# Softmax halves put off behind the next maximum, values between a second head's scores, and an early row load in an attention stage

## The chip, the cores and the metric

The kernel runs on one core of a Trainium2 chip. The metric is the device time of one execution in microseconds (us). A core has a matrix engine (PE), a vector engine (DVE, VectorE), a scalar engine (ACT, ScalarE), GpSimd (POOL) and a sync engine (SP) that here only issues transfers. Each engine works through its own list of instructions in order; semaphores order the engines among each other. Matmul results land in PSUM, which has eight banks of 128 partitions x 512 f32.

## What is computed

One inference step of two layers on 256 prompt tokens and 1024 latent tokens of width 1024. The first layer is a gated linear attention, the second a softmax attention with 8 heads over 2 key/value heads; the change lies in the second. Cut to what matters here:

```python
def attend_blocks(q, keys, vals):               # one block of 128 queries
    def one(qblk):
        s = jnp.einsum("bqhgd,bkhd->bhgqk", qblk, keys).astype(jnp.float32) * scale
        p = jax.nn.softmax(s, axis=-1).astype(vals.dtype)
        return jnp.einsum("bhgqk,bkhd->bqhgd", p, vals)

# layer 1, latent tokens: 1024 own keys and 256 cached ones
qs, ks_, vs, gs = attn_project(hs, att_w_in[i], att_qnorm[i], att_knorm[i])
out_s = (attend_blocks(rope_2d(qs), keys, vals) * jax.nn.silu(gs)) @ att_w_out[i]
xs = xs + gt_s * out_s
```

The prompt tokens do the same over their own 256 keys.

## The kernel before

Every f32 product is made of three f16 matmuls: an operand is split into a high and a low half, and hi x hi, hi x lo and lo x hi add up in one PSUM bank.

The attention stage (`attention`) runs 10 steps: two groups of four heads (p) times five column blocks c of 256 tokens. Block 0 holds the prompt (256 keys), blocks 1 to 4 the latent tokens (1280 keys). In each step the four heads e = 0 to 3 are taken in order, and each head has two halves j of 128 tokens. A score tile is one head's half: `scores` computes 128 x 1280 scores with nine matmuls into an S tile of three banks, of which there are two. Then come the maximum over the row (VectorE, line 977), its scaled negative (ScalarE, 979), the exponential with its row sum (ScalarE, 982), the reciprocal of the sum and that times 2**14 (VectorE, 984 and 986), the high half of the normalised row (GpSimd, 989), the low half (VectorE, 990), and one transposing transfer of both halves into PT, issued by SP (991). `values` multiplies a head's PT with the values, two heads late: a list `pend` holds the two heads that wait. The row buffers p and phl exist twice, PT three times.

Between the scores of an even head stands the projection of the next queries (`query`, 24 matmuls); its norm, rotary turn and split go to ScalarE, VectorE, GpSimd and SP, the second half of them in the odd head (`query_rest`). After an odd head, `gateT` computes the gate of both heads of the pair (2 x 24 matmuls), and its SiLU runs on ScalarE and VectorE (`silu`, `logsig`, lines 224 to 235). All these matmuls use two `mm` banks. So a pair of heads is four score tiles, one query projection, two `values` and two gates. The last step has no queries left to project.

`out2_prep` loads a block's finished attention rows back from DRAM (line 1086) and splits them for the output projection, with a maximum over the rows (1090), a small matmul that spreads it over the partitions (84), and the split on ScalarE (1097) and VectorE (1098). For the first output block it is called in the second head of the last step. After the loop come the first tile of the output projection (`out_tile`), the last two `values`, and `att_out` with the other nine tiles.

The engines' lists are not in the order of the program text: the framework's scheduler reorders independent instructions by a time model of its own, and `tc.issue_after(x)` holds the instructions of a block on x's engine behind x. In the code of before nothing in the attention stage is held in that way.

Before the attention stage, `gla_out` fills the PSUM with pools y, tr, mm and kv of two banks each, whose first banks are taken in the order y, tr, mm, kv (line 1309). The attention's pool is laid over the same eight banks: the two S tiles over the first six, its `mm` over the last two. A bank is reused when the old tile's last reader is through.

Of the kernel before, what the change touches and what calls it, by code (L numbers as in the profile page):

```python
# [16 lines left out]
P = 128  # L17
# [9 lines left out]
HD, AH, KVH = 128, 8, 2  # L27
# [16 lines left out]
OUT = (1, 0, 2, 3, 4)  # L44
# [8 lines left out]
class K:  # L53
# [907 lines left out]
    def scores(self, h, c, j, q, PT):  # L961
        nc = self.nc
        kv = h // (AH // KVH)
        nk = 256 if c == 0 else TS + PAST
# [12 lines left out]
        nc.vector.tensor_reduce(mx, S, AX.X, ALU.max)  # L977
# [4 lines left out]
        nc.scalar.activation(p, S, AF.Exp, scale=self.sexp, bias=nb, accum_out=den)  # L982
        r = self.t(self.sm, [P, 1], F32, "srec")
# [59 lines left out]
    def attention(self, wo):  # L1043
        self.S0 = self.t(self.ps, [P, 1536], F32, "S")
        wq, wg, q, g = self.wq, self.wg, self.q, {}
        pend, later = [], []
        for n, (p, c) in enumerate(self.steps):
# [8 lines left out]
            for e in range(4):  # L1056
                h = 4 * p + e
                if later:
                    self.nc.sync.dma_start(*later.pop(0))
                PT = self.t(self.sp, [P, 20, 256], F16, "PT", bufs=3)  # L1060
                self.scores(h, c, 0, q[(p, c, 0)], PT)
                if e % 2 == 0:
                    self.query()
                else:
                    self.query_rest()
                self.scores(h, c, 1, q[(p, c, 1)], PT)
                if len(pend) == 2:
                    self.values(*pend[0], g.pop(pend.pop(0)[0]))
                pend.append((h, c, PT))
                if e % 2 == 1:  # L1070
                    g.update({i: self.gateT(i, c, *wg[p]) for i in (h - 1, h)})
                if n == 9 and e == 1:
                    first = self.ropet.rearrange("p a b d -> p (a b d)").bitcast(F16)
                    first = first.rearrange("p (j h t) -> p j h t", j=2, h=AH)
                    self.prep = self.out2_prep(OUT[0], (first[:, 0], first[:, 1]))
# [7 lines left out]
    def out2_prep(self, c, parts):  # L1083
        nc = self.nc
        og = self.t(self.wst, [P, AH, 256], F32, "wst")
        nc.sync.dma_start(og, self.og2_d[c])
# [42 lines left out]
def emit(ctx, tc, I, O, dbg=None, stop=None):  # L1129
# [172 lines left out]
    with ExitStack() as ca:  # L1302
        k.ap = k.pool("ap", ctx=ca, side="right")
        with ExitStack() as c:
# [4 lines left out]
            k.held = {t: k.bank(t) for t in ("y", "tr", "mm", "kv")}  # L1309
# [110 lines left out]
```

## Time and profile before

| quantity | value |
| --- | --- |
| median of 3 runs (lowest, highest) | 1352.31 us (1348.84, 1357.2) |
| the profiled execution: its time | 1360.72 us |
| the profiled execution: its span | 1358.9 us |
| mean granted clock of the matrix engine | 0.978 |
| first score matmul of the attention stage | 784.83 us |
| first matmul of the output projection's second block | 1260.76 us |

The span is what the profile covers; the execution's time has 1.8 us around it. In the profile's lines a time is counted from the start of the span, a row of the timeline reads "start, duration, engine, line, operation, out<-in, shape", and in brackets at its end stands how long the engine sat idle before it and what released it. Lines name the tile, not its number. "PEld" is the load of a stationary operand, which runs beside the matmuls. Neighbouring matmuls overlap in the records, so the cost of one is read from start to start.

### The profile page before, as it was taken

How to read it: one execution, taken by the hardware profiler on the slowest of the kernel's cores; microseconds unless marked ns; L12 is line 12 of the kernel's file. 1: busy time of each engine (PE TensorE's matmuls, PEld its weight loads, DVE VectorE, ACT ScalarE, POOL GpSimd, SP SyncE). 2: the span in 40 equal slices, each digit the busy share in tenths (PEclk: the TensorE clock that was granted, in tenths of full speed). 3: DMA queues.
4: the chain of work that ended last, by engine and by line, in shares of the span. 5: the costliest groups of instructions: out<-in, count | busy, mean ns of one | idle time of the engine just before them, and what ended most of it. 6: DMA issues, size and time to landing. Idle time of an engine off the chain costs nothing. (4 is left out here: it accounts for less than half of the span.)

```text
span 1358.9 us, 22664 instructions
## 1 busy us (share of the span) xinstructions
PE 1245.7 (92%) x8150; PEld 808.9 (60%) x8150; DVE 931.1 (69%) x2138; ACT 669.7 (49%) x1661; POOL 382.8 (28%) x623
## 2 busy tenths in 40 slices
PE   4789999999999999697889989899999989989998
PEld 2357765655555556475657656666676756665444
DVE  1776868886867788755654567777768677875552
ACT  2565646655646567523323455555566555562110
POOL 1232212422322133401222534333233343422000
PEclk9899999999999999898989999999999989999999
DMA  9612455544545532377543268576859638887532
GB/s 306 219 62 95 140 178 182 168 154 133 187 132 178 160 113 78 101 214 198 129 127 121 60 181 155 104 137 121 188 102 188 128 83 145 182 156 171 174 132 78
DMA packets 344769, 199.14 MB, mean 147 GB/s; under 512 B 229406, under 2 KB 331534, under 8 KB 343376
## 3 DMA queue, kind: packets, MB, share of 16 engines
q1 hardware_dynamic: 297024, 159.67, 47.3%
q10 hardware_dynamic: 47312, 37.25, 8.5%
q8 instruction: 64, 1.05, 0.3%
q0 software_dynamic: 320, 0.77, 0.2%
q14 instruction: 49, 0.40, 0.1%
HBM read 104.31 MB, written 37.24 MB: 104 GB/s over the span
## 5 line engine op out<-in xcount | busy, mean ns | idle before, releaser
L125 PE MATMUL mm<-whi,hT_hi 128*128 128x512 f16 (+1 forms) x560 | 197.1, 352 | 12.1 <-ACT gx L471 7.4
L125 PEld LDWEIGHTS <-hT_hi 128*128 128x128 f16 x1440 | 142.2, 99 | 109.9 <-issue 15.4
L125 PE MATMUL mm<-wlo,hT_hi 128*128 128x512 f16 (+1 forms) x560 | 196.8, 351 | 0.0
L125 PE MATMUL mm<-whi,hT_lo 128*128 128x512 f16 (+1 forms) x560 | 196.6, 351 | 0.0
L125 PEld LDWEIGHTS <-whi 128*128 128x128 f16 x1368 | 135.5, 99 | 90.5 <-issue 21.7
L125 PE MATMUL mm<-hT_hi,whi 128*128 128x256 f16 (+1 forms) x512 | 155.2, 305 | 10.5 <-DVE og L1015 5.4
L989 POOL TENSOR_SCALAR phl<-p,srec 128x1280 f16<-128x1280 f32 (+1 forms) x80 | 99.9, 1250 | 218.7 <-DVE srec L984 146.2
L125 PE MATMUL mm<-hT_lo,whi 128*128 128x256 f16 (+1 forms) x512 | 155.5, 304 | 0.2 <-DVE hT_lo L350 0.2
L125 PE MATMUL mm<-hT_hi,wlo 128*128 128x256 f16 (+1 forms) x512 | 155.4, 304 | 0.0
L990 DVE SCALAR_TENSOR_TENSOR phl<-p,srec,phl 128x1280 f16<-128x1280 f32 (+1 forms) x80 | 107.5, 1344 | 59.0 <-POOL phl L989 58.9
L974 PE MATMUL S<-kT,wst 128*128 128x512 f16 (+1 forms) x624 | 122.9, 338 | 14.4 <-ACT p L982 14.4
L125 PE MATMUL mm<-PT,vh 128*128 128x256 f16 x672 | 113.7, 273 | 4.9 <-DMA PT<-phl 4.5
L977 DVE TENSOR_REDUCE smx<-S 128x1 f32<-128x1280 f32 (+1 forms) x80 | 101.0, 1267 | 3.3 <-PE S L974 3.3
L982 ACT ACTIVATE p<-S,snb,sexp 128x1280 f32<-128x1280 f32 (+1 forms) x80 | 99.3, 1241 | 5.0 <-DVE srec L984 1.1
L125 PEld LDWEIGHTS <-hT_lo 128*128 128x128 f16 x720 | 71.1, 99 | 49.7 <-issue 1.0
L974 PEld LDWEIGHTS <-wst 128*128 128x128 f16 x624 | 61.0, 98 | 65.8 <-issue 16.2
L125 PEld LDWEIGHTS <-wlo 128*128 128x128 f16 x720 | 71.3, 99 | 39.6 <-issue 2.8
L125 PE MATMUL mm<-PT,vl 128*128 128x256 f16 x336 | 91.6, 273 | 0.0
L125 PE MATMUL y<-whi,ogT 128*128 128x256 f16 (+1 forms) x336 | 76.6, 318 | 6.7 <-DVE xr L724 4.6
L147 DVE TENSOR_REDUCE wmx<-wst 128x1 f32<-128x512 f32 x104 | 64.5, 676 | 26.5 <-DMA wst<-in_gla_w_in 10.7
L979 ACT ACTIVATE snb<-smx,nsexp 128x1 f32<-128x1 f32 x80 | 23.4, 292 | 115.7 <-DVE smx L977 115.7
L125 PEld LDWEIGHTS <-vh 128*128 128x128 f16 x672 | 65.4, 98 | 15.0 <-issue 4.3
(335 smaller groups left out, 2696.8 us busy)
## 6 DMA issues: line engine op xcount, KB each, us to landing
wada<-in_w_ada SPq DMA_DIRECT2D x16, 1024.0 KB, 5.0
wst<-in_gla_w_in SPq DMA_DIRECT2D x12, 1024.0 KB, 5.8
wst<-in_att_w_in SPq DMA_DIRECT2D x10, 1024.0 KB, 8.3
xr<-x_d SPq DMA_DIRECT2D x11, 512.0 KB, 3.3
og_d<-gx ACTq DMA_DIRECT2D x40, 128.0 KB, 1.8
og_d<-og ACTq DMA_DIRECT2D x40, 128.0 KB, 3.8
wst<-og_d SPq DMA_DIRECT2D x5, 1024.0 KB
out<-xr ACTq DMA_DIRECT2D x17, 256.0 KB, 2.0
```

The source lines that it names most:

```text
L125: self.nc.tensor.matmul(out, a, b, start=k == 0 and j == 0, stop=k == n - 1 and j == 2)
L147: nc.vector.tensor_reduce(mx[:, j : j + 1], st[:, 2 * j : 2 * j + 2, :], AX.XY, ALU.max, apply_absolute_value=True)
L974: nc.tensor.matmul(S[:, a : a + n], x, y, start=m == 0, stop=m == 2)
L977: nc.vector.tensor_reduce(mx, S, AX.X, ALU.max)
L979: nc.scalar.activation(nb, mx, AF.Copy, scale=self.nsexp)
L982: nc.scalar.activation(p, S, AF.Exp, scale=self.sexp, bias=nb, accum_out=den)
L989: nc.gpsimd.tensor_scalar(hi, p, r, 2.0 ** 14, ALU.mult, ALU.mult)
L990: nc.vector.scalar_tensor_tensor(lo, p, r2, hi, ALU.mult, ALU.subtract)
```

## The change

The softmax of a score tile is cut in two. `scores` now ends with the exponential and keeps the rest (reciprocal, high half, low half, transposing transfer) in `self.put_off`; the next call of `scores` emits that rest behind its own maximum, held behind it on VectorE by `issue_after`. After the loop one last `rest()` takes the last tile. In an odd head the call of `values` moves from behind the second score tile to between the two. The load of the first output block is split off `out2_prep` (`out2_load`) and called in the first head of the last step; the rest of `out2_prep` is held behind the maximum of the second head's second tile. And `gla_out`'s banks are taken in the order y, tr, kv, mm, so that the attention's `mm` lies over the old `mm` and its second S tile over the old kv.

```diff
--- before.py
+++ after.py
@@ -974,12 +974,26 @@
                 nc.tensor.matmul(S[:, a : a + n], x, y, start=m == 0, stop=m == 2)
             a += n
         mx = self.t(self.sm, [P, 1], F32, "smx")
-        nc.vector.tensor_reduce(mx, S, AX.X, ALU.max)
+        last = nc.vector.tensor_reduce(mx, S, AX.X, ALU.max).ins
         nb = self.t(self.sm, [P, 1], F32, "snb")
         nc.scalar.activation(nb, mx, AF.Copy, scale=self.nsexp)
         p = self.t(self.sp, [P, TS + PAST], F32, "p")[:, 0:nk]
         den = self.t(self.sm, [P, 1], F32, "sden")
         nc.scalar.activation(p, S, AF.Exp, scale=self.sexp, bias=nb, accum_out=den)
+        self.rest(last)
+        self.last = last
+        self.put_off = p, den, PT, j, nk
+
+
+    def rest(self, after=None):
+        if self.put_off is None:
+            return
+        if after is not None:
+            with self.tc.issue_after(after):
+                return self.rest()
+        nc = self.nc
+        p, den, PT, j, nk = self.put_off
+        self.put_off = None
         r = self.t(self.sm, [P, 1], F32, "srec")
         nc.vector.reciprocal(r, den)
         r2 = self.t(self.sm, [P, 1], F32, "srec2")
@@ -1041,7 +1055,7 @@
             self.queries_out(self.half.pop(), 1)
 
     def attention(self, wo):
-        self.S0 = self.t(self.ps, [P, 1536], F32, "S")
+        self.S0, self.put_off = self.t(self.ps, [P, 1536], F32, "S"), None
         wq, wg, q, g = self.wq, self.wg, self.q, {}
         pend, later = [], []
         for n, (p, c) in enumerate(self.steps):
@@ -1061,18 +1075,24 @@
                 self.scores(h, c, 0, q[(p, c, 0)], PT)
                 if e % 2 == 0:
                     self.query()
+                    self.scores(h, c, 1, q[(p, c, 1)], PT)
                 else:
                     self.query_rest()
-                self.scores(h, c, 1, q[(p, c, 1)], PT)
                 if len(pend) == 2:
                     self.values(*pend[0], g.pop(pend.pop(0)[0]))
+                if e % 2 == 1:
+                    self.scores(h, c, 1, q[(p, c, 1)], PT)
                 pend.append((h, c, PT))
                 if e % 2 == 1:
                     g.update({i: self.gateT(i, c, *wg[p]) for i in (h - 1, h)})
+                if n == 9 and e == 0:
+                    row = self.out2_load(OUT[0])
                 if n == 9 and e == 1:
                     first = self.ropet.rearrange("p a b d -> p (a b d)").bitcast(F16)
                     first = first.rearrange("p (j h t) -> p j h t", j=2, h=AH)
-                    self.prep = self.out2_prep(OUT[0], (first[:, 0], first[:, 1]))
+                    with self.tc.issue_after(self.last):
+                        self.prep = self.out2_prep(row, (first[:, 0], first[:, 1]))
+        self.rest()
         gt = self.t(self.wst, [P, KT, 256], F32, "wst").rearrange("p (i k) n -> p i (k n)", i=2)
         self.fold_gate(1, wo[0][2] + wo[1][2], gt)
         wo[:] = [(hi, lo, 512) for hi, lo, _ in wo]
@@ -1080,10 +1100,13 @@
         for t in pend:
             self.values(*t, g.pop(t[0]))
 
-    def out2_prep(self, c, parts):
-        nc = self.nc
+    def out2_load(self, c):
         og = self.t(self.wst, [P, AH, 256], F32, "wst")
-        nc.sync.dma_start(og, self.og2_d[c])
+        self.nc.sync.dma_start(og, self.og2_d[c])
+        return og
+
+    def out2_prep(self, og, parts):
+        nc = self.nc
         hi, lo = parts
         mx = self.t(self.small, [P, 2], F32, "wmx")
         for j in range(2):
@@ -1113,7 +1136,7 @@
         w = self.wtile(0)
         for n, c in enumerate(OUT):
             if n + 1 < 5:
-                nxt = self.out2_prep(OUT[n + 1], [t[:, :, 256 * (n % 2) : 256 * (n % 2) + 256] for t in w[0:2]])
+                nxt = self.out2_prep(self.out2_load(OUT[n + 1]), [t[:, :, 256 * (n % 2) : 256 * (n % 2) + 256] for t in w[0:2]])
             for j in range(n == 0, 2):
                 x = self.t(self.xp, [P, D], F32, "xr")
                 self.out_tile(c, j, x, wo, (512, 256, 256) if (n, j) == (4, 1) else (512, 512))
@@ -1306,7 +1329,7 @@
             k.hw = k.pool("hw3", bufs=2, ctx=c)
             k.sm = k.pool("sm3", bufs=4, ctx=c)
             k.ps = k.pool("ps3", 2, PSUM, c)
-            k.held = {t: k.bank(t) for t in ("y", "tr", "mm", "kv")}
+            k.held = {t: k.bank(t) for t in ("y", "tr", "kv", "mm")}
             k.p2_bank = "kv"
             k.gla_out(wo, prep, (k.nw, k.w2))
         if "x1" in k.dbg:
```

No instruction is added to or taken from the arithmetic. What follows are rows of the engines' lists, of before and of the changed kernel.

VectorE, from the second head's first tile of one pair to the first tile of the next pair (step 1). Names: smx is a tile's maximum, srec its reciprocal, phl the normalised halves, xhl a query's split, ls and gx the gate. Before, phl_10139 and phl_10185 are the two tiles of the odd head, smx_10302 the maximum of the next pair:

```order
L986 TENSOR_SCALAR srec_2381_10137<-srec_10135 128x1
L990 SCALAR_TENSOR_TENSOR phl_10139<-p_10132,srec_2381_10137,phl_10139 128x1280
L984 RECIPROCAL srec_10181<-sden_10179 128x1
L849 TENSOR_TENSOR xhl_10160<-hx_2356_10009,xhl_10160 128x256
L986 TENSOR_SCALAR srec_2395_10183<-srec_10181 128x1
L227 SCALAR_TENSOR_TENSOR ls_10250<-gx_10248,ls_10250 128x256
L990 SCALAR_TENSOR_TENSOR phl_10185<-p_10178,srec_2395_10183,phl_10185 128x1280
L235 TENSOR_TENSOR gx_10248<-gx_10248,ls_10250 128x256
L977 TENSOR_REDUCE smx_10302<-S_10292 128x1
L227 SCALAR_TENSOR_TENSOR ls_10284<-gx_10282,ls_10284 128x256
L235 TENSOR_TENSOR gx_10282<-gx_10282,ls_10284 128x256
L984 RECIPROCAL srec_10309<-sden_10307 128x1
```

The same place in the changed kernel (phl_10211 and phl_10305 are the odd head's tiles, smx_10294 the next pair's maximum):

```order
L1004 SCALAR_TENSOR_TENSOR phl_10211<-p_10124,srec_2394_10209,phl_10211 128x1280
L849 TENSOR_TENSOR xhl_10152<-hx_2353_10001,xhl_10152 128x256
L227 SCALAR_TENSOR_TENSOR ls_10242<-gx_10240,ls_10242 128x256
L977 TENSOR_REDUCE smx_10294<-S_10284 128x1
L998 RECIPROCAL srec_10301<-sden_10205 128x1
L235 TENSOR_TENSOR gx_10240<-gx_10240,ls_10242 128x256
L227 SCALAR_TENSOR_TENSOR ls_10276<-gx_10274,ls_10276 128x256
L1000 TENSOR_SCALAR srec_2409_10303<-srec_10301 128x1
L1004 SCALAR_TENSOR_TENSOR phl_10305<-p_10204,srec_2409_10303,phl_10305 128x1280
L235 TENSOR_TENSOR gx_10274<-gx_10274,ls_10276 128x256
```

The low half of the pair's last tile and its reciprocal stood ahead of the next pair's maximum and now stand behind it; in the changed kernel it is so with every tile, while the list of before had it so only in places (such as an even head's second tile, whose low half already stood behind the next maximum).

The matrix engine, end of the same odd head's second score tile. mm_10189 (before) is a `values` with the odd head's PT of the pair before; S_10164 is the score tile:

```order
L974 MATMUL S_10164<-kT_7577,wst_9068 128x256
L974 LDWEIGHTS wst_9068
L974 MATMUL S_10164<-kT_7577,wst_9068 128x256
L125 LDWEIGHTS vl_7579
L125 MATMUL mm_10189<-PT_9809,vl_7579 128x256
L125 LDWEIGHTS vh_7578
L125 MATMUL mm_10189<-PT_9809,vh_7578 128x256
```

In the changed kernel (mm_10215 is the first gate of the pair):

```order
L974 MATMUL S_10190<-kT_7577,wst_9068 128x256
L974 LDWEIGHTS wst_9068
L974 MATMUL S_10190<-kT_7577,wst_9068 128x256
L125 LDWEIGHTS whi_2167_9060
L125 MATMUL mm_10215<-hT_hi_71,whi_2167_9060 128x256
L125 LDWEIGHTS whi_2167_9060
L125 MATMUL mm_10215<-hT_lo_72,whi_2167_9060 128x256
```

Before, 11 of the 30 matmuls of these values stand ahead of the score tile and 19 behind it; now all 30 stand ahead of it and the gates follow. The list of a pair is thus score, 24 of the query, score, 30 of values, score, 30 of values, score, 48 of the gates.

VectorE in the second step with prompt tokens (the seventh step). wmx and wm are the row maximum of `out2_prep` for the first output block, og the result of a `values`:

```order
L990 SCALAR_TENSOR_TENSOR phl_13246<-p_13239,srec_3006_13244,phl_13246 128x256
L227 SCALAR_TENSOR_TENSOR ls_13154<-gx_13152,ls_13154 128x256
L1090 TENSOR_REDUCE wmx_14827<-wst_14825 128x1 x2
L235 TENSOR_TENSOR gx_13152<-gx_13152,ls_13154 128x256
L1094 TENSOR_TENSOR wm_3321_14830<-wmx_14827 128x1
L1015 SCALAR_TENSOR_TENSOR og_13257<-mm_13250,inv_o_7592,gx_13118 128x256
L977 TENSOR_REDUCE smx_13266<-S_13262 128x1
L977 TENSOR_REDUCE smx_13306<-S_13302 128x1
```

In the changed kernel:

```order
L1000 TENSOR_SCALAR srec_2987_13168<-srec_13166 128x1
L1004 SCALAR_TENSOR_TENSOR phl_13170<-p_13074,srec_2987_13168,phl_13170 128x256
L227 SCALAR_TENSOR_TENSOR ls_13146<-gx_13144,ls_13146 128x256
L235 TENSOR_TENSOR gx_13144<-gx_13144,ls_13146 128x256
L977 TENSOR_REDUCE smx_13227<-S_13223 128x1
L998 RECIPROCAL srec_13234<-sden_13164 128x1
L1000 TENSOR_SCALAR srec_3003_13236<-srec_13234 128x1
L1029 SCALAR_TENSOR_TENSOR og_13249<-mm_13242,inv_o_7592,gx_13110 128x256
L977 TENSOR_REDUCE smx_13258<-S_13254 128x1
L1004 SCALAR_TENSOR_TENSOR phl_13238<-p_13163,srec_3003_13236,phl_13238 128x256
```

The reduction over the loaded rows stood here, three steps ahead of its call, and now stands in the last step, behind the maximum of the second head's second tile. The load of these rows on SP's list stays in the seventh step; it moved ahead of one of the odd head's two transposing transfers, behind both of which it stood.

More of the change, by code (lines that the diff above doesn't have):

```diff
@@ L1081, in attention @@
             self.values(*t, g.pop(t[0]))
-    def out2_prep(self, c, parts):
+    def out2_load(self, c):
+        og = self.t(self.wst, [P, AH, 256], F32, "wst")
+        self.nc.sync.dma_start(og, self.og2_d[c])
+        return og
+    def out2_prep(self, og, parts):
         nc = self.nc
-        og = self.t(self.wst, [P, AH, 256], F32, "wst")
-        nc.sync.dma_start(og, self.og2_d[c])
         hi, lo = parts
```

## Prediction

> **What bounds the kernel now.** I read the page's table of engines first, then the windows of the attention stage, the waits of the matrix engine in it, the windows of single pairs, and then the timeline around each wait.
>
> ```profile
> PE 1245.7 (92%) x8150; PEld 808.9 (60%) x8150; DVE 931.1 (69%) x2138; ACT 669.7 (49%) x1661; POOL 382.8 (28%) x623
> 784.80:1262.10 477.30, 443.07 (x3105) 304.66 (x3104) 351.61 (x673) 264.94 (x669) 170.05 (x238) 0.99 0.73 145
> PE S L974 <- ACT p L982: 14.4, 10, 2.1
> PE mm L125 <- DVE og L1015: 5.4, 5, 3.6
> PE mm L125 <- ACT rope L930: 4.6, 1, 4.6
> PE mm L125 <- DMA PT<-phl: 4.5, 4, 2.2
> PE S L125 <- ACT whi L1097: 2.3, 1, 2.3
> PE mm L125 <- DVE srec L986: 1.7, 6, 0.3
> PE S L125 <- DVE wlo L1098: 0.7, 1, 0.7
> PE mm L125 <- PE S L974: 0.4, 1, 0.4
> 926.19:952.40 26.21, 23.78 (x169) 16.43 (x168) 19.27 (x36) 14.15 (x35) 8.38 (x11) 1.00 0.65 121
> sum 127.43, PE 119.01 PEld 82.23 DVE 95.21 ACT 70.35 POOL 43.78; mean PE 23.80 PEld 16.45 DVE 19.04 ACT 14.07 POOL 8.76
> ```
>
> First the whole kernel, then the stage (its length, then the busy time of PE, PEld, DVE, ACT and POOL with their instructions, the granted clock, the DMA share, GB/s). The matrix engine is busy 443.07 of 477.30 us, so at most the 34.2 between them can be won, and a slower clock on top. The waits (us, times, longest) name that time: the ten of 14.4 are the score matmul that waits for the exponential that reads its S tile, and the change is aimed at them. One pair takes 26.21 us where the matrix engine has 23.78 and VectorE 19.27: the matrix engine is the bound with some 10% of slack, and VectorE is next. The last row sums five pairs from 850.35 on: 127.43, 25.5 a pair.
>
> What a pair costs without waits follows from pitches:
>
> ```profile
> 835.14 0.38 PE L125 MATMUL mm<-whi,hT_hi 128*128 128x512 f16 x1
> 840.32 1.79 PE L974 MATMUL S<-kT,wst 128*128 128x512 f16 x9
> 841.94 0.38 PE L125 MATMUL mm<-PT,vh 128*128 128x256 f16 x2
> 845.21 1.78 PE L974 MATMUL S<-kT,wst 128*128 128x512 f16 x9
> 854.04 0.27 PE L125 MATMUL mm<-hT_hi,whi 128*128 128x256 f16 x1
> 856.66 1.24 PE L974 MATMUL S<-kT,wst 128*128 128x512 f16 x5
> ```
>
> Start to start: a query's 24 matmuls take 840.32 − 835.14 = 5.18, a score tile 1.62, the 30 of a `values` 3.27, a gate's 24 take 2.62. A pair is 5.18 + 4 x 1.62 + 2 x 3.27 + 2 x 2.62 = 23.4. The stage holds 20 pairs: 16 with 1280 keys and 4 with 256; the last step's two pairs have no query.
>
> **The change, part by part.**
>
> *Steady pairs.* Before, 11 of 30 values matmuls (1.2 us) separate the odd head's score tiles, too few for the tile's maximum and exponential; now all 30 (3.27) do, and 5.2 of gates follow. These are the rows of the softmax (min/median/max in ns, then first and last start):
>
> ```profile
> L977 DVE TENSOR_REDUCE smx<-S x80: 407/1478/1493, 793.0 to 1228.1; 128x1 f32<-128x1280 f32 x64, 128x1 f32<-128x256 f32 x16
> L982 ACT ACTIVATE p<-S,snb,sexp x80: 544/1417/1422, 794.9 to 1231.7; 128x1280 f32<-128x1280 f32 x64, 128x256 f32<-128x256 f32 x16
> L979 ACT ACTIVATE snb<-smx,nsexp 128x1 f32<-128x1 f32 x80 | 23.4, 292 | 115.7 <-DVE smx L977 115.7
> L989 POOL TENSOR_SCALAR phl<-p,srec x80: 475/1334/2101, 796.7 to 1240.0; 128x1280 f16<-128x1280 f32 x64, 128x256 f16<-128x256 f32 x16
> L990 DVE SCALAR_TENSOR_TENSOR phl<-p,srec,phl x80: 469/1550/1630, 801.2 to 1241.5; 128x1280 f16<-128x1280 f32 x64, 128x256 f16<-128x256 f32 x16
> DMA to landing us min/median/max: 2.4/5.3/9.4
> ```
>
> An S tile is free after maximum 1.48, scale 0.29 and exponential 1.42, 3.2 us plus the time until VectorE takes it up. With two S tiles, what a tile waits for is the tile two back: the odd head's second tile waits for the even head's second, which ended 3.27 + 1.62 + 3.27 = 8.2 before; every other interval is as long or longer (the shortest is again 8.2, or 5.2 + 1.62 + 3.3). So the ten waits go: 14.4, of which 2.1 is the last step's (costed there), leaves 12.3. A low half (1.55) that VectorE used to finish first no longer stands ahead of the maximum. The 1.7 of waits of a gate's bank for `srec` goes too, for the gates now begin behind a score tile and not behind values whose bank is just being read; so do the four shorter ones for `og` (5.4 − 3.6 = 1.8). Gain 15.8.
>
> In place of them stands a new wait. The odd head's `values` reads the PT of the pair's last tile before, whose rest now begins only behind the next pair's first maximum. From that tile's end: gates 5.24 and score 1.62 = 6.86; then maximum 1.48, reciprocal and scale 0.3, high half 1.33 on GpSimd, low half 1.55 on VectorE, the transfer 5.3 (median above), and some 0.5 of semaphores and issue: 17.3. The values start 5.24 + 1.62 + 5.18 + 1.62 + 3.27 + 1.62 = 18.6 after it. The slack is 1.3, on the median landing, and VectorE's list has two gate operations between the reciprocal and the low half. I read no wait of this kind for it in before's rows, so I bound it: none (slack kept) to 3.2 a pair (a landing of 8.45, the slowest row of the last step below). I take 0.33 a pair, nearer the median landing: 14 full pairs with a query, 4.7. **A: 15.8 − 4.7 = 11.1.**
>
> *Start.* Below stand the query's first matmul behind ScalarE (the bracket: idle before, and for what), the first maximum, and the second score tile:
>
> ```profile
> 790.70 0.47 ACT L930 ACTIVATE rope<-kv,inv_av 128x256 f32<-128x256 f32 x1 [3.54 <-DMA out<-rope]
> 791.22 0.58 PE L125 MATMUL mm<-whi,hT_hi 128*128 128x512 f16 x1 [4.61 <-ACT rope L930]
> 793.01 1.48 DVE L977 TENSOR_REDUCE smx<-S 128x1 f32<-128x1280 f32 x1
> 797.89 1.79 PE L974 MATMUL S<-kT,wst 128*128 128x512 f16 x9
> ```
>
> The attention's first `mm` bank lies over an old kv bank, which line 930 reads last. With mm and kv exchanged it lies over the old mm, free earlier, and the second S tile over kv, not written before 5.2 us later. The wait of 4.61 goes, and with it a slow start: the 24 matmuls took 797.89 − 791.22 = 6.67, not 5.18, 1.5 more: 6.1. But the first maximum starts at 793.01 behind other VectorE work whatever the matrix engine does, and its exponential ends at about 793.0 + 3.2 = 796.2; the third tile, which needs it, would be due at 797.89 + 1.62 − 6.1 + 1.2 = 794.6, 1.6 too early. At least 1.7 is given back there, and up to all 6.1, since VectorE has more to do in this stretch than the matrix engine; I take 3.0. **B: 6.1 − 3.0 = 3.1.**
>
> *Seventh step.* The scheduler had placed `out2_prep`'s row maximum (1090) ahead of an `og`:
>
> ```profile
> 1089.02 2.35 DVE L1090 TENSOR_REDUCE wmx<-wst 128x1 f32<-128x1024 f32 x2 [3.44 <-DMA wst<-og_d]
> 1092.21 0.37 PE L125 MATMUL mm<-hT_hi,whi 128*128 128x256 f16 x1 [3.62 <-DVE og L1015]
> 1100.29 1.78 PE L974 MATMUL S<-kT,wst 128*128 128x512 f16 x9
> 1092.00:1096.00 4.00, 3.79 (x18) 2.60 (x18) 3.09 (x13) 2.15 (x10) 2.48 (x7) 0.50 0.19 66
> ```
>
> VectorE sat 3.44 idle for the load and then 2.35 in it; `og` stood behind it, and the gate's bank behind `og`: 3.62. After that stall the granted clock was 0.50 for 4 us, and the 48 gate matmuls took 1100.29 − 1092.21 = 8.08 instead of 5.24. Both go: 3.62 + 2.84. In the last step the same 2.35 stand behind the head's second maximum, with rows loaded long before; VectorE has no query work there, and the next score tile is 5.2 of gates away. The load itself moves on SP's list ahead of one transposing transfer of 256 keys; the low half that transfer needs now comes later than the load can be issued, so cost 0, up to 3.6 (one wait like the one above) if not. **C: 6.4.**
>
> *Last step.* Its waits before, the three transfers on the chain of waits and the score's wait:
>
> ```profile
> 1200.88 1.78 PE L974 MATMUL S<-kT,wst 128*128 128x512 f16 x9 [2.11 <-ACT p L982]
> 1207.27 5.87 DMA PT<-phl
> 1216.24 5.19 DMA PT<-phl
> 1231.43 8.45 DMA PT<-phl
> ```
>
> Before: 2.1 for S, 4.5 for PT, and 2.3 + 0.7 at the end for the output's halves, 9.6. After: without a query a pair is 5.2 shorter, so the new PT wait bites. From the end of the even head's first tile to the odd head's values stand values and two scores, some 22 x 0.109 + 3.2 = 5.6, while maximum 1.6, low half 1.55 and landing 5.3 need 8.5: 2.9; two heads on, with one more piece of work between, 1.3. The output's halves are split earlier, and 17 matmuls (3.7) of values stand ahead of the first matmul that reads them, so 2.3 + 0.7 go. **D: 9.6 − 4.2 = 5.4.**
>
> *Weight loads beside transposes.* The loads of weights stay where they are in SP's list, but with transposes issued later more of them fall beside a load. The one of 8.45 was such a one, 3.2 above the median. Four loads lie in the loop; bounds 0 and 4 x 3.2 less a slack of 1.3 each, 7.6; I take 0.5 for each. **F: −2.**
>
> GpSimd's queue: the high half now stands behind the query's turn where that is due first (at most 4 x 0.33); covered by VectorE's own gate work, cost 0, and 1.3 without that cover, inside R1's price.
>
> Sum: 11.1 + 3.1 + 6.4 + 5.4 − 2 = 24.0. The profiled execution took 1360.7 (span 1358.9 and 1.8 around it), 8.4 above the median; 24 off it is 1336.7, and off the median of 1352.3 it is 1328.3, so 1328.
>
> **The two engines that share.** These rows are a high half on GpSimd and a VectorE addition that runs into it, and the same addition without it:
>
> ```profile
> 901.67 1.55 POOL L989 TENSOR_SCALAR phl<-p,srec 128x1280 f16<-128x1280 f32 x1
> 902.06 1.44 DVE L838 TENSOR_TENSOR hx<-hx,rope 128x256 f32<-128x256 f32 x1
> 908.43 0.40 DVE L838 TENSOR_TENSOR hx<-hx,rope 128x256 f32<-128x256 f32 x1
> ```
>
> The addition lasts 1.44 instead of 0.40 and ends 0.28 after the high half (903.50 against 903.22): it was held until GpSimd was through. Most such time was time in which VectorE would have waited for the high half anyway; where it wouldn't, each collision costs up to 1.03. The Trainium skill, "SBUF — State Buffer", section "Who interferes with whom", says that a VectorE instruction with two SBUF inputs and a GpSimd instruction that reads SBUF lock each other out, the first to issue keeping the shared port; the trace agrees by the rows above. It speaks against this change, which leaves VectorE's other work running beside the high half: with four collisions a pair by that rule, the sum would be R1's.
>
> **The rivals.**
> - *R1, the new wait is real (same side or none).* Landings of 6.8 instead of 5.3, or the four collisions at 1.03 in VectorE's way, put the odd head's values 1.5 to 4 late. At a landing of 6.8 a pair is 25.0, A is about −1 and the net about 12 to 13: 1340. With all four collisions a pair is as long as before, and 4 are left: 1348. For it: slack of only 1.3, and 8.45 does occur. Against it: the median is 5.3, and VectorE is only 19.3 busy of 23.4.
> - *R2, all waits go.* Transposes in time, the start kept whole, nothing lost in the last step: 15.8 + 6.1 + 6.4 + 9.6 = 38, 1314. For it: VectorE's slack; against it: the first maximum at 793.01.
> - *R3, slower: the transfer bounds the pair.* If transposes land after 8.45 on average, each pair waits 3.2 and takes 26.7, against 25.5 in the 8 pairs that waited before and, by estimate, 24.1 (the work and some 0.7 of small waits) in the other 6: 8 x 1.2 + 6 x 2.6 = 25 lost, 3 more in the last step, against B + C + D = 15: 13 slower, 1365. It decides from a pair of about 25.8, a mean landing of 7.6. Against it: of the three rows above two are under 5.9.
> - *The change doesn't do what it says.* The lists of both engines show the matmuls and the halves moved, so I give this no chance.
>
> **How the numbers follow.** Forecast 0.55, R2 0.15, R1 0.22, R3 0.08. The range goes from R2's end to between R1's two ends, 1313 to 1346, leaving out R3, a slower part of R1 and little beyond R2. A measurement of this kernel can tell about 1% from no change, 13.5 us: faster means below 1338.8, all of forecast and R2 but a few hundredths, and a small part of R1: 0.73. R1's rest and a little of R3 lie within 1%: 0.21. Slower: 0.06.
>
> **What would show it.** Waits of the score for the exponential in the stage: none or under 2 us (A's first part); waits for PT: about 5 us in all in the loop and about 4 in the last step; a pair at 23.5 to 24, its VectorE busy at 19.3 as before. The first query's matmul starts before 788 and the 24 take under 6.7. No reduction 1090 and no clock of 0.50 near 1090; that reduction in the last step with no idle ahead of it. The median landing of PT stays near 5.3. Wrong would make it: waits for PT above 15 us in all, a low half over 1.6, a median landing above 6.5, or a score that waits for a maximum which VectorE takes up late.

## The result and the profile after

| | median us | range | executions |
| --- | --- | --- | --- |
| before | 1353.20 | 1348.84 to 1362.39 | 20 |
| changed | 1345.18 | 1341.26 to 1354.90 | 20 |

The ratio of the changed kernel to the one before is 0.9945 (95% interval 0.9924 to 0.9965): 7.4 us faster, by 4.7 to 10.3. The forecast was 24 us, so the sign was right and the size three times too large. An execution more than 1.5% above the fastest of its kernel isn't counted in a ratio; in the series below that leaves out one of `d_firstonly` and one of before beside it.

The profiled execution of the changed kernel took 1341.58 us, near the fast end of its range, with a span of 1339.8, 19.1 below the span of before's trace. That isn't the change's worth: 8.8 of it were there before the attention stage began, in a stretch that the change leaves alone but for the order of the banks (first score at 776.01 against 784.83; in the same kernel's second trace it is at 780.90, and in the other traces of this study between 778 and 786). So I count from the first score.

The waits of the matrix engine in the stage (us, times, longest) answer to the list shown of before:

```profile
PE mm L125 <- DMA PT<-phl: 13.5, 9, 4.0
PE mm L125 <- issue: 3.7, 1, 3.7
PE S L974 <- ACT p L982: 3.6, 2, 2.5
PE mm L125 <- ACT snb L979: 3.1, 1, 3.1
PE S L125 <- DVE p L724: 1.2, 1, 1.2
PE mm L125 <- DMA whi<-w_g: 1.0, 1, 1.0
```

The score's wait for the exponential fell from 14.4 to 3.6, and those for `og` and for the rope (5.4 and 4.6) are gone. The wait for PT grew from 4.5 to 13.5; the second and fourth row belong to it too, for both are a `values` that reads PT (the trace names another releaser). So some 20 us of waits for PT stand where 4.5 stood.

Where they are is seen from points that both kernels pass with the same matrix work done: the starts of the loop's queries, q1 to q18. Two belong to each of the first nine steps; the prompt steps are the fifth (q9, q10) and the seventh (q13, q14). First the timeline's rows of before (first score, q9, q14, q15, q17; q3 at 835.14 stands in the prediction), then of the changed kernel (first score, q3, q9, q14, q15, q17):

```profile
784.83 1.79 PE L974 MATMUL S<-kT,wst 128*128 128x512 f16 x9
987.68 0.38 PE L125 MATMUL mm<-whi,hT_hi 128*128 128x512 f16 x1
1081.28 0.38 PE L125 MATMUL mm<-whi,hT_hi 128*128 128x512 f16 x1
1101.91 0.38 PE L125 MATMUL mm<-whi,hT_hi 128*128 128x512 f16 x1
1144.18 0.38 PE L125 MATMUL mm<-whi,hT_hi 128*128 128x512 f16 x1
```

```profile
776.01 1.79 PE L974 MATMUL S<-kT,wst 128*128 128x512 f16 x9
823.75 0.38 PE L125 MATMUL mm<-whi,hT_hi 128*128 128x512 f16 x1
964.30 0.38 PE L125 MATMUL mm<-whi,hT_hi 128*128 128x512 f16 x1
1068.53 0.38 PE L125 MATMUL mm<-whi,hT_hi 128*128 128x512 f16 x1
1082.87 0.38 PE L125 MATMUL mm<-whi,hT_hi 128*128 128x512 f16 x1
1130.00 0.38 PE L125 MATMUL mm<-whi,hT_hi 128*128 128x512 f16 x1
```

The differences by stretch, and the same from a second trace of the changed kernel (run re_after below):

| stretch | work in it | gained us | second trace |
| --- | --- | --- | --- |
| first score to q3 | start, first step | 2.6 | 1.4 |
| q3 to q9 | six full pairs | 12.0 | 12.2 |
| q9 to q14 | prompt step, sixth step, begin of the seventh | -10.6 | -6.7 |
| q14 to q15 | rest of the seventh step | 6.3 | 6.3 |
| q15 to q17 | eighth step | -4.9 | -5.0 |
| q17 to the end | ninth step, last step, output | 4.9 | 5.6 |
| sum | | 10.3 | 13.9 |

A full pair in the middle now runs without a wait (window from q6 to q7; length, then the engines' busy time, granted clock, DMA share, GB/s):

```profile
894.74:918.20 23.46, 23.46 (x170) 16.45 (x168) 18.64 (x34) 12.74 (x33) 11.94 (x14) 1.00 0.76 134
```

So the gain is there, and three places hand most of it back. The first is q9 to q10, 5.8 us longer than before (2.7 in the second trace). These are timeline rows of the stretch ahead of it and of the wait:

```profile
949.99 1.03 SPq L1073 DMA_DIRECT2D whi<-w_g  x2
951.07 1.58 SPq L1073 DMA_DIRECT2D wlo<-w_g  x2
953.33 6.77 SPq L1005 DMA_TRANSPOSE PT<-phl  x1
963.58 1.33 POOL L1003 TENSOR_SCALAR phl<-p,srec 128x1280 f16<-128x1280 f32 x1 [5.51 <-DMA PT<-phl]
964.94 1.55 DVE L1004 SCALAR_TENSOR_TENSOR phl<-p,srec,phl 128x1280 f16<-128x1280 f32 x1 [3.63 <-POOL phl L1003]
977.74 0.59 PE L125 MATMUL mm<-PT,vh 128*128 128x256 f16 x2 [4.01 <-DMA PT<-phl]
```

Four pieces of a weight load (2 MB) are issued within 2.7 us; the transpose behind them holds SP for 6.77. Its row buffer stays taken, so the next high half waits 5.51 on GpSimd, VectorE waits 3.63 for that, the next transposes are late in turn, and the last tile's PT lands 4.01 late. After the wait the clock is low:

```profile
949.99:964.00 14.01, 14.01 (x118) 11.20 (x116) 9.27 (x21) 7.18 (x14) 5.65 (x5) 1.00 1.04 252
977.74:983.79 6.05, 6.05 (x30) 4.36 (x31) 3.12 (x10) 1.28 (x4) 2.55 (x7) 0.53 0.28 65
```

While the weights move, the transfer engines are full (share 1.04). Behind the wait, 30 values matmuls take 6.05 instead of 3.27 at a granted clock of 0.53: the wait costs 6.8, not 4. Before the change the transfer engines were as full behind the same load, issued from 969.51 on, and no `values` waited for PT there:

```profile
969.50:983.50 14.00, 12.89 (x104) 10.02 (x103) 11.08 (x19) 8.05 (x21) 4.35 (x4) 1.00 0.99 243
```

The second place is q11 to q12, 3.0 us longer (2.3 in the second trace), and it too stands behind a load:

```profile
1004.92 1.01 SPq L1073 DMA_DIRECT2D whi<-w_o  x2
1006.02 0.85 SPq L1073 DMA_DIRECT2D wlo<-w_o  x2
1008.32 2.69 SPq L1005 DMA_TRANSPOSE PT<-phl  x1
1016.15 0.38 PE L125 MATMUL mm<-PT,vh 128*128 128x256 f16 x2 [3.10 <-ACT snb L979]
1087.08 1.22 SPq L1005 DMA_TRANSPOSE PT<-phl  x1
```

The transpose at 1008.32 moves the prompt step's last tile, whose rest is put off into the next step. The `values` that read it start at 1016.15, 7.8 later, after a wait of 3.10. At 1087.08 stands the same transpose behind the other prompt step, with no weights beside it; its `values` don't wait.

The third place is the eighth step:

```profile
1082.87:1101.09 18.22, 18.22 (x123) 11.74 (x121) 15.42 (x30) 11.91 (x31) 7.63 (x13) 1.00 0.42 77
1101.09:1130.00 28.91, 25.26 (x171) 17.22 (x168) 23.86 (x42) 15.84 (x39) 12.31 (x15) 0.94 0.80 137
1099.46 1.79 PE L974 MATMUL S<-kT,wst 128*128 128x512 f16 x9
1102.57 1.40 DVE L227 SCALAR_TENSOR_TENSOR ls<-gx,ls 128x256 f32<-128x256 f32 x1
1104.23 1.54 DVE L1004 SCALAR_TENSOR_TENSOR phl<-p,srec,phl 128x1280 f16<-128x1280 f32 x1
1105.69 1.48 DVE L977 TENSOR_REDUCE smx<-S 128x1 f32<-128x1280 f32 x1
1116.60 0.59 PE L125 MATMUL mm<-PT,vh 128*128 128x256 f16 x2 [3.65 <-issue]
```

The pair behind a prompt step multiplies PTs of 256 keys, so it has 18.22 us of matrix work where a full one has 23.46, and four full softmax tiles all the same. VectorE falls behind: the tile scored from 1099.46 to 1101.1 gets its maximum at 1105.69, 4.6 late, behind two put-off halves (the second one is shown). The put-off half of the tile before it (scored from 1095.22) stands behind this maximum, and so that tile's PT is 3.65 late for the odd head's `values` in the pair from q16 on.

### The profile page after: what moved, and what is told of

The parts are those of the page before. It is cut to its first block, busy times and chain, and to the rows that moved or that the text cites. A ratio compares the mean times of both kernels' runs of the same rounds, so it can differ in the third digit from the quotient of the medians.

```text
span 1339.8 us, 22669 instructions
## 1 busy us (share of the span) xinstructions
PE 1240.6 (93%) x8150; PEld 808.5 (60%) x8150; DVE 928.7 (69%) x2138; ACT 662.8 (49%) x1661; POOL 402.0 (30%) x623
## 5 line engine op out<-in xcount | busy, mean ns | idle before, releaser
L1003 POOL TENSOR_SCALAR phl<-p,srec 128x1280 f16<-128x1280 f32 (+1 forms) x80 | 106.4, 1330 | 198.6 <-DVE srec L998 106.6
L125 PE MATMUL mm<-PT,vh 128*128 128x256 f16 x672 | 118.4, 281 | 20.2 <-DMA PT<-phl 13.5
L977 DVE TENSOR_REDUCE smx<-S 128x1 f32<-128x1280 f32 (+1 forms) x80 | 101.5, 1270 | 11.0 <-PE S L974 10.9
L125 PE MATMUL mm<-PT,vl 128*128 128x256 f16 x336 | 94.5, 281 | 0.0
```

The source lines that it names most:

```text
L125: self.nc.tensor.matmul(out, a, b, start=k == 0 and j == 0, stop=k == n - 1 and j == 2)
L977: last = nc.vector.tensor_reduce(mx, S, AX.X, ALU.max).ins
L1003: nc.gpsimd.tensor_scalar(hi, p, r, 2.0 ** 14, ALU.mult, ALU.mult)
```

## The experiments

All ratios are against the kernel before in the same series. "From q3 to q9" and the like are the stretches above, each from that run's trace against before's.

**The parts alone.** The exchange of banks:

```diff
-            k.held = {t: k.bank(t) for t in ("y", "tr", "mm", "kv")}
+            k.held = {t: k.bank(t) for t in ("y", "tr", "kv", "mm")}
```

> Only the order in which the stage before takes its banks is changed (y, tr, kv, mm). The prediction's terms: 3.1 us faster, the matrix engine's wait of 4.61 us for ScalarE ahead of the first query gone and the first score to the second score in 6.8 us instead of 13.1. Rival, that the start is bound by VectorE: the wait goes in the trace, the same time comes back as waits for the exponential or for PT in the first two pairs, and the time is the same within 1 us.

Measured 0.9986 (0.9966 to 1.0006). The wait of 4.61 is gone and q1 gains 4.8; by q3 3.2 of it is left and the stage as a whole gains 2.8. Near the forecast of 3.1 in the trace; by the times it can't be told from nothing.

The output rows' load split off and the rest held behind the last step's maximum (the two hunks with `row`, `self.last` and `out2_load`):

```diff
+                if n == 9 and e == 0:
+                    row = self.out2_load(OUT[0])
...
-                    self.prep = self.out2_prep(OUT[0], (first[:, 0], first[:, 1]))
+                    with self.tc.issue_after(self.last):
+                        self.prep = self.out2_prep(row, (first[:, 0], first[:, 1]))
```

> Only the output block's row load is split off and the rest of that preparation held behind the maximum in the last step. The prediction's terms: the wait of 3.62 us in the seventh step and its slow clock go, 6.4 us faster. Rival, that the stall covers other work that is then waited for (transposes that queue on SP): under 3 us faster, with waits for PT in the seventh and eighth step that the kernel before doesn't have.

Measured 0.9964 (0.9943 to 0.9985), 4.9 us. From q14 to q15 it gains 6.6, as forecast, and no wait takes its place at that point.

The move of the values matmuls:

```diff
                 if e % 2 == 0:
                     self.query()
+                    self.scores(h, c, 1, q[(p, c, 1)], PT)
                 else:
                     self.query_rest()
-                self.scores(h, c, 1, q[(p, c, 1)], PT)
                 if len(pend) == 2:
                     self.values(*pend[0], g.pop(pend.pop(0)[0]))
+                if e % 2 == 1:
+                    self.scores(h, c, 1, q[(p, c, 1)], PT)
```

> Only the values matmuls of an odd head stand between its two score tiles; the softmax isn't cut. The prediction's terms: of the 14.4 us of waits for the exponential under 4 are left, and 3 of the small bank waits go too, so 10 to 15 us faster; no new wait for PT, since the second half of a softmax isn't put off. Rival, that the deferral is what frees the maximum: over 8 us of waits for the exponential are left, at most 5 us faster.

Measured 0.9986 (0.996 to 1.0012). Its waits:

```profile
PE mm L125 <- DVE og L1015: 11.3, 11, 1.6
PE S L974 <- ACT p L982: 4.3, 5, 1.9
```

The waits for the exponential went as the first theory said, from 14.4 to 4.3, and the time didn't follow: what the score no longer waits, a bank waits for `og`, 11.3 instead of 5.4. VectorE was still late, and another instruction met it. From q3 to q9 it gains 1.3.

The deferral alone (`scores` and `rest` as in the changed kernel, all else as before):

> Only the second half of a tile's softmax is put off behind the next maximum. The prediction's terms: with 11 values matmuls between the odd head's scores half of the 14.4 us of waits stays, and the last step's waits for PT come in: 2 to 5 us faster. Rival, that a put-off transpose meets the weight loads on SP's queue: waits for PT of 10 us or more, near the steps in which weights are loaded, and the time is the same or up to 5 us longer.

Measured 0.9975 (0.9946 to 1.0004). Waits for the exponential 2.5 although the values stand where they stood; waits for PT 19.5 in ten places. From q3 to q9 it gains 12.9, from q9 to q14 it loses 10.8. Both theories met half of it: the deferral carries the whole gain of the full pairs, and the loss as well.

**The changed kernel without the move of the values:**

> The changed kernel without the move of the values matmuls. If the move brings what the prediction gave it: waits for the exponential of 5 us or more come back and the time is 4 to 8 us longer than the changed kernel's. If the deferral alone frees the score tiles, as its single run showed (waits for the exponential 2.5 us): the same within 2 us, or up to 4 us faster because the prompt steps keep their old order.

Measured 0.9947 (0.9922 to 0.9971), the changed kernel's ratio; 13.1 gained from q3 to q9. The move brings nothing once the halves are put off.

**Two theories of the late transposes.** L: they meet the weight loads. S: prompt steps have too little matrix work to cover a put-off half. For L, each piece of a later weight load is held behind a transpose of its own head (`self.moved` is the last tile's transpose):

```diff
-                if later:
-                    self.nc.sync.dma_start(*later.pop(0))
...
                 pend.append((h, c, PT))
+                if later:
+                    with self.tc.issue_after(self.moved):
+                        self.nc.sync.dma_start(*later.pop(0))
```

> The changed kernel with the four pieces of each later weight load held one per head on SP, each behind a transpose of that head, instead of all together where the scheduler put them. If the waits for PT come from transposes that queue behind weights (theory L): the waits of 4.0 us in the fourth step's end, with the slow clock behind it, and of 3.0 us at the last step's begin go, waits for PT in the stage 5 us or less, 6 to 10 us faster than the changed kernel. If they come from too little matrix work in the prompt steps (theory S): the waits there stay, at most 3 us faster.

Measured 0.9852 (0.9822 to 0.9883). The wait of 4.01 and its slow clock are gone, and q9 to q14 costs 0.4 instead of 10.6; the wait of 3.10 at q11 to q12 is gone as well, though the prompt step's halves are put off as before (1.5 of its 3.0 come back in the next pair, in a wait of 1.79). The last step's wait of 2.96 stays (2.97), so that one isn't the loads'. The edit does two things at once: it spaces the pieces (the first of these loads is issued from 980.6 to 1005.4 instead of 949.99 to 952.7), and with that it moves them from ahead of q9 to behind it, into the prompt step, whose transposes move a fifth of the data. Which of the two frees the transposes wasn't tried apart.

For S, nothing is put off in the prompt steps nor out of the step ahead of them:

```diff
         self.put_off = p, den, PT, j, nk
+        if c == 0 or (j and h % 4 == 3 and self.near):
+            self.rest()
```

> The changed kernel, with nothing put off in the two steps with prompt tokens nor out of the step ahead of them. Theory S (a pair of small tiles has some 15 us of matrix work between a tile's end and the values that read it, a put-off half needs 17): the waits for PT around these steps go and the two prompt steps get 5 to 9 us shorter, 5 to 9 us faster than the changed kernel. Theory L: the waits stay within 2 us, since the weight loads stay where they are.

Measured 0.9883 (0.9864 to 0.9901). The time is 8 us below that of the changed kernel by the ratios, but the trace shows little of it: q9 to q14 still costs 7.8, with a wait of 4.24 where 4.01 was; only the stretch q11 to q12 gets its 3 us back, and the next one loses 1.3 of them. S isn't what the wait of 4 us comes from. The 3 us behind the prompt step go with either edit, and the other prompt step, with its halves put off and no load beside them, hasn't that wait: it takes both, a put-off half and a load.

Both edits:

> The changed kernel with both edits: weight loads one per head, and nothing put off in and into the prompt steps. If both causes are there, the gains add: 8 to 15 us faster than the changed kernel, about 1332 us. If one of the two makes the other idle, no faster than the better of the two.

Measured 0.9861 (0.9837 to 0.9885): no better than the loads alone. The gains don't add, as they wouldn't if one load makes both waits.

**The start, the first pair behind a prompt step, and controls.** The kernel with the loads held, but those of the first step left where they were (against `a_spread`):

```diff
+                if later and n == 0:
+                    self.nc.sync.dma_start(*later.pop(0))
...
-                if later:
+                if later and n:
                     with self.tc.issue_after(self.moved):
```

> The changed kernel with the weight loads of the fifth, seventh and tenth step held one per head on SP, the first step's load left where it was (one per head there had added some 6 us of waits in the first two pairs). Theory L: about 5 us faster than with all four loads held, 16 us faster than the changed kernel. Rival, that the start's waits come back whatever the load does: the same as with all four held.

Measured 0.9895 (0.9868 to 0.9922), no gain over holding all four: my reading of the start was wrong (last section).

To this, nothing put off in the first pair behind each prompt step:

```diff
         self.put_off = p, den, PT, j, nk
+        if self.at_once:
+            self.rest()
...
+                self.at_once = n in (5, 7) and e < 2
```

> That kernel, and nothing put off in the first pair behind each of the two prompt steps, where the matrix engine has 18 us of work and VectorE 19. If the put-off half causes the wait of 3.0 to 3.7 us in the eighth step: it goes with the slow clock behind it, 3 to 6 us faster than the kernel with the loads alone. If VectorE is late there in either order: no gain.

Measured 0.9826 (0.98 to 0.9853), 1333.05 us in the median, the fastest of all, 1.7% below before (20 us by the medians). Its window from q16 to q17, ahead of it the same of the kernel without this edit:

```profile
1101.39:1128.46 27.07, 23.80 (x171) 16.29 (x169) 23.41 (x41) 14.96 (x37) 13.54 (x15) 1.00 0.87 143
1098.51:1122.65 24.14, 23.61 (x170) 16.37 (x168) 21.97 (x38) 15.04 (x38) 12.00 (x14) 1.00 0.88 149
```

The pair is 2.9 us shorter, and the wait is gone.

The three later loads held in the kernel before:

> The kernel before with the same three weight loads held one per head. Theory L says that the transposes of before had room for the loads, and only the put-off half makes them late: the same within 2 us as before. If the loads cost the same without the change: 6 us or more faster than before.

Measured 1.0032 (1.0006 to 1.0059). Holding the loads gains nothing without the deferral, and no `values` of before waited at them: L holds only together with the put-off half.

The changed kernel again:

> The changed kernel once more, on the chip of the runs beside it: 0.990 to 0.998 of before, with a wait for PT of about 4 us at the fourth step's end and one of 3 to 4 us in the eighth step again. If those waits were chance, they stand elsewhere.

Measured 0.9944 (0.9921 to 0.9968). The eighth step's wait stands in the same place at 3.7; that at the fourth step's end was 2.29, so its place is fixed and its size isn't.

**What was still open.** The first pairs' edit without the loads held:

> The changed kernel, with nothing put off in the first pair behind each of the two prompt steps, and the weight loads where they were. If that pair's late halves cost by themselves what the two kernels with loads held showed (4.7 us in the eighth step): the wait of 3 to 4 us there goes, 4 to 7 us faster than the changed kernel, and the wait of 4 us at the fourth step's end stays.

Measured 0.9912 (0.9881 to 0.9943), eleven of its twelve executions from 1332 to 1349. The eighth step's wait fell to 1.89 and q15 to q17 loses 1.5 instead of 4.9; the wait at the fourth step's end was 2.16, about that of the changed kernel's second trace. In the trace the edit works by itself, less fully; by the times it isn't clear of the changed kernel.

The changed kernel with its weight loads on ScalarE's queue:

```diff
-                    self.nc.sync.dma_start(*later.pop(0))
+                    self.nc.scalar.dma_start(*later.pop(0))
```

> The changed kernel with the later weight loads issued by ScalarE's queue instead of SP's, at nearly the same time. If the transposes are late because they stand behind the weights in one queue: the 4 us at the fourth step's end go as they did with one load per head, 4 to 8 us faster than the changed kernel. If they share the transfer engines' throughput whatever the queue: that wait stays within 1 us.

Measured 1.005 (1.002 to 1.008), slower than before. The waits of the `values` after two of the loads:

```profile
968.31 0.58 PE L125 MATMUL mm<-PT,vh 128*128 128x256 f16 x2 [7.74 <-DMA PT<-phl]
1183.48 0.58 PE L125 MATMUL mm<-PT,vh 128*128 128x256 f16 x2 [8.84 <-issue]
```

The transposes don't stand behind the weights in one queue any more and are later than ever, so that order isn't what makes them late. What is left, and fits a share of 1.03 from 954 to 968, is the shared transfer engines; a ScalarE held up by issuing the loads isn't the reason, for its next exponential starts 0.6 behind the end of its maximum (957.80 against 957.20). These loads are also issued 2.7 us earlier in their pair. The expectation's second cause fits, but not its number: the wait didn't stay within 1 us, it almost doubled. The Trainium skill, "DMA: Bandwidth & Descriptors", section "Queues, rings and completion order", says that each transfer engine takes turns between the queues that have work for it; these two rows agree with it, for a second queue then takes its turns from the transposes instead of passing ahead of or behind them.

Nothing put off in the last step either, on top of the fastest kernel (`self.at_once = n in (5, 7) and e < 2 or n == 9`):

> The kernel with loads held and nothing put off in the first pairs behind prompt steps, and nothing put off in the last step either, which has no query to cover it. If the last step's waits for PT (2.97, 0.8 and 1.2 us) are the put-off half's: they go, but up to 2.1 us of waits for the exponential come back, 1 to 4 us faster than without this edit. If the transfer's own time sets them: the same within 1 us.

Measured 0.9873 (0.984 to 0.9906), not faster. The wait of 2.9 stays: it reads the PT of the ninth step's last tile, which this edit leaves put off.

A third buffer for the rows (phl), which would cut the chain from a late transpose to the next high half, wasn't tried: there is no room for it.

## Why the prediction was right and wrong

**Steady pairs (A), right in kind, wrong in its reach.** For the six full pairs from q3 to q9 the working gives 11.1 us of waits removed (9.0 for the exponential, 2.1 for banks) less 6 x 0.33, 9.1; 12 were measured, with one wait for PT of 0.45 in six pairs. The slack of 1.3 held. But I credited the distance of 30 matmuls; the runs of the parts show that the deferral gains it all and the move nothing. What had been late was VectorE, with a low half ahead of each maximum.

**The step that failed** is the term for "weight loads beside transposes", with "I take 0.5 for each": F was -2, and the stretch q9 to q14, which holds the loads of two steps, lost 10.6 and 6.7; 8.8 and 5.0 of that are the two stretches behind the loads, q9 to q10 and q11 to q12. I thought of one transpose beside a load. In truth 2 MB fill the transfer engines, the two row buffers pass the delay on from tile to tile, and a slow clock follows. With the loads held the same stretch lost 0.4; whether by the spacing or by the place is open. Before the change no tile's transpose was put off by rule, and the same loads held up no `values`.

A second step failed with it: in the chain of 17.3 the next tile's maximum starts at that tile's end ("then maximum 1.48"). In the full pairs that is nearly so (a first tile scored from 869.04 to 870.7, its maximum at 871.25). The first pair behind a prompt step has 18.2 us of matrix work instead of 23.5 and the same four softmax tiles, and in the eighth step the maximum began 4.6 late. Less the slack of 1.3 that is 3.3, near the wait of 3.65. The run that doesn't put off that pair, with the loads held, loses 0.1 from q15 to q17 instead of 4.9. The prediction had named waits for PT above 15 us and a maximum which VectorE takes up late as what would make it wrong; there were some 20 us, and this maximum.

**Start (B):** 3.1 forecast, 2.6 and 1.4 measured, 2.8 alone. The give-back was sized about right.

**Seventh step (C):** 6.4 forecast, 6.3 measured in both traces, 6.6 alone.

**Last step (D):** the wait forecast as 2.9 was 2.96 and the one of 1.3 was 0.8, but 1.2, 1.1 and 1.2 stood beside them that I hadn't seen. From q17 to the end, which also holds the ninth step, 4.9 and 5.6 were gained. That 2.9 was met is luck:

```profile
1175.30 1.78 PE L974 MATMUL S<-kT,wst 128*128 128x512 f16 x9
1179.24 1.48 DVE L977 TENSOR_REDUCE smx<-S 128x1 f32<-128x1280 f32 x1
1190.79 0.39 PE L125 MATMUL mm<-PT,vh 128*128 128x256 f16 x2 [2.96 <-DMA PT<-phl]
```

The sum has 8.5 us from the tile's end to the landing, without the high half (1.33) and the reciprocal that the chain of 17.3 counts, and 5.6 until the `values`. The tile ended at 1175.30 + 1.62 = 1176.9; its maximum began 2.3 late, the PT was there 13.9 after the tile's end, and the `values` were due after 10.9. Both terms were some 5 us too short, and only their difference was right.

**The rivals.** R1, the new wait being real, came nearest (1340 and 1348, measured 1345), but not by its mechanism, and its prices are too high: they leave out the slack of 1.3, and so do R3's 3.2 and A's upper bound. By the prediction's own chain a landing of 6.8 is 0.2 late, not 1.5, and one of 8.45 is 1.9 late. Nor did its mechanism show: the median landing of PT hardly moved (5.5, was 5.3), and the lock between VectorE and GpSimd cost the full pairs no visible time (no wait, VectorE busy 18.64 in the pair shown). It shows where VectorE was late already: the gate's operation of 1.40 at 1102.57, which mostly takes 0.41, beside a high half. The rule of the Trainium skill ("SBUF — State Buffer", section "Who interferes with whom") agrees with that row. R3 named the place, a transfer that is late behind loads, but spread it over all pairs.

**Trace and median.** The two traces give 10 and 14 us, the times 7.4. Both profiled executions lie near the fast end of theirs; what the slower ones hold no trace shows. With loads held and first pairs at once six executions lie within 1329 to 1336, with the loads where they were (d_firstonly) eleven of twelve within 1332 to 1349. This speaks for the loads, and isn't shown.

## What to carry to other kernels

A slack worked out for the steady body of a loop must be worked out again for each irregular step and for the one behind it, where less matrix work leaves VectorE behind and the chain begins late. When work is put off, look up what bulk transfers share its engines and how many buffers hang on its landing: the stretch with two loads lost 7 to 11 us here with the pieces together, and 0.4 with one piece per head, which also came later. A wait that an edit removes is only gained if the engine that was late does less: moving matmuls between two scores changed who waited.

## What was not expected of the hardware

The granted clock after like waits differed. Around the first step's PT the changed kernel (second trace) waited 2.5 and 1.4 us and kept a clock of 1.00; with the later loads held (`c_spread3`, where the first step's are left as they were), it waited 2.5 and 0.9 and had 0.69 in the 8 us behind (first row the changed kernel's, then the other's):

```profile
820.00:828.00 8.00, 8.00 (x73) 6.90 (x71) 6.55 (x11) 4.21 (x8) 6.17 (x6) 1.00 0.46 94
820.00:828.00 8.00, 7.45 (x49) 5.86 (x50) 4.51 (x11) 2.50 (x5) 3.54 (x3) 0.69 0.43 87
```

Between q2 and q3 the kernels with loads held lost 4.2 to 7.0 us, the changed kernel 2.5 and 3.2, which is why I first blamed the load of the first step. `d_firstonly`, whose loads aren't held, lost 4.2 too, so it isn't the loads. The Trainium skill, "TensorE: Matmul & The Clock Gate", section "Part 1: The HAM clock gate", says that the clock follows activity in a window that runs by itself, so that the same matmuls can meet it in another phase. The two rows would agree with that; no run here shows the window, and what decided between them is open.

Moving transfers to another queue made the transposes later, not earlier (7.74 against 4.01).
